# Strassen quarters for the i and z projections of heads 4 to 15, placed one product at a time among the t blocks

## The chip, the cores and the metric

One core of one Trainium2 chip runs the whole kernel in one launch. The metric is device time in microseconds (us). A core has a matrix engine (TensorE, PE in the profile; its weight loads are PEld), VectorE (DVE), ScalarE (ACT), GpSimd (POOL), the queue engine SyncE (SP), and 16 DMA engines that they share. Matmul results go to PSUM, which has eight banks of 128 x 512 floats here.

## The reference

A two-layer encoder on x of 512 tokens x 1024, in float32. Layer 0 is a gated MLP beside windowed attention. Layer 1, on which the change bears:

```
h = rms_norm(x, norm_g_odd);  proj = h @ w_in_odd              # 1024 -> 5 x 2048
q, f_f, f_b, i, z = split(proj)                                # 16 heads of 128 each
per head, both directions: f = lb + (1-lb)*sigmoid(f_logit), k = 1-f, in chunks of 64:
    S_t = diag(f_t) S_{t-1} + k_t outer i_t,   o_t = S_t^T silu(q_t)
o = rms_norm per head(o_fwd + o_bwd) * head_norm_g
x = x + (o * silu(z)) @ w_out_odd;   out = rms_norm(x, final_norm_g)
```

## The kernel before, in words

Every float32 product of a projection is made of three matmuls: each operand is split into a rounded high part and a low rest (hi, lo), and hi*hi, hi*lo and lo*hi are summed in PSUM (`mm3`, L212). One 128 x 128 by 128 x 512 step so costs three matmuls.

Weights come in pieces of 128 partitions x 1024 floats (512 KB) through `Weights` (L33). The list of pieces is written down once (L294 to L323) in the order of use. `take` hands out the next piece; `ahead` keeps up to 7 pieces requested and 3 split. A piece is loaded by SP into one of 4 `wraw` buffers (L55), ACT rounds it into `whi` (L66), and DVE subtracts to get `wlo` (L67); `whi` and `wlo` have 4 buffers each, so a split can wait for the matmuls that read an older piece.

Layer 1 goes in four groups J of four heads. For each group: `nat_blocks` computes i, then z, for the group's 512 columns (4 token tiles, 8 steps of three matmuls = 24 matmuls each; ACT copies i, L775; ACT sigmoid and DVE multiply make silu(z), L778 and L779); groups 1 and 2 then add the output projection of the group before (`out_blocks`, L260, added to x by DVE, L279); then each head computes q, f and b transposed (`t_block`, L220, 24 matmuls each, evacuated by ACT sigmoids, L790 and L794) and spawns `hgrn(h)` (L657). All these big blocks take their PSUM bank from the four-deep tag "mm" (L105); the heads' small matmuls use four "sm" banks.

`hgrn` is a generator. Its six pauses are counted in ticks: after every 8 matmuls of `mm3` one tick (L217) lets up to three such side jobs emit their next part. POOL has four steps in it: a memset (L663), the sum of two masked products (L708), the power -1/2 of the norm (L150), and the multiplication by silu(z) (L758). The written order is the priority; the framework's planner then puts each engine's instructions in the order in which its cost model finds them ready, and each engine runs its own list strictly in order.

After the last group come the output projections of heads 8 and 9, 10 to 13, and `last_blocks` (L799) with heads 14 and 15 and the final norm. The chip's first work is a chain on ACT: the first `hhi` (L348) and the first weight pieces.

Of the kernel before, what the change touches and what calls it, by code (L numbers as in the profile page):

```python
# [32 lines left out]
class Weights:  # L33
# [3 lines left out]
    def __init__(self, tc, pool, dma_ahead, split_ahead, raw_bufs, bufs):  # L37
        self.tc, self.nc, self.pool = tc, tc.nc, pool
        self.dma_ahead, self.split_ahead = dma_ahead, split_ahead
        self.raw_bufs, self.bufs = raw_bufs, bufs  # L40
        self.src, self.raw, self.ready = [], {}, {}
        self.n_dma = self.n_split = self.n_used = 0
        self.halved = 0

    def add(self, ap):
        self.src.append(ap)

    def _dma(self):
# [44 lines left out]
def tile_encoder(ctx, tc, x, xT, nge, wie, lng, lnb, ws, bs, sink, woe, ngo, wio, gaf, gab, hng, woo, fng, out):  # L93
# [17 lines left out]
    W = Weights(tc, wp, dma_ahead=7, split_ahead=3, raw_bufs=4, bufs=4)  # L111
# [171 lines left out]
    def act_pair():  # L283
        return [act.tile([P, S], F32R, tag=n, name=n, bufs=8) for n in ("ahi", "alo")]
# [38 lines left out]
    add_out(woo, 14, 2)  # L323

    with ExitStack() as c0:
# [95 lines left out]
        def layer_norm(t):  # L421
# [8 lines left out]
            nc.vector.tensor_tensor(out=va[t], in0=va[t], in1=lngb, op=ALU.mult)  # L430
            nc.gpsimd.tensor_tensor(out=va[t], in0=va[t], in1=lnbb, op=ALU.add)
# [338 lines left out]
    for J in range(4):  # L770
        iv = l1.tile([P, NT, 512], F32, tag="iv", name="iv", bufs=2)
        zv = l1.tile([P, NT, 512], F32, tag="zv", name="zv", bufs=2)
# [8 lines left out]
        nat_blocks(evac_i)  # L781
        nat_blocks(evac_z)
        if J in (1, 2):
            tick_until(lambda: 4 * J - 1 in acat1)
            out_blocks([acat1[4 * (J - 1) + k] for k in range(4)])
        for h in range(4 * J, 4 * J + 4):
            sq = l1.tile([P, 2, S], F32, tag="sq", name="sq", bufs=3)
            sg = l1.tile([P, 2, S], F32, tag="sg", name="sg", bufs=3)
# [106 lines left out]
```

## Time and profile before

| | |
|---|---|
| median of 3 runs | 1028.81 us (1028.78 to 1029.21) |
| the profiled execution's own time | 1028.67 us |
| its span, first to last instruction | 1027.0 us, so 1.67 us lie outside it |
| granted TensorE clock, mean | 0.998 |
| busy share PE, DVE, ACT, POOL | 98%, 59%, 51%, 13% |

Busy time of PE counts pipelined matmuls from their start to a modelled end, so matmuls overlap in it; the distance between two starts is what one costs. The other engines' busy time is occupancy. "DMA share" is the mean busy share of the core's 16 DMA engines.

### The profile page before, as it was taken

Reading aid. Unit: us, or ns where it says so; the run is one execution under the profiler, and the core shown is the slowest. Engines: PE = TensorE matmul, PEld = TensorE weight load, DVE = VectorE, ACT = ScalarE, POOL = GpSimd, SP = SyncE. Lnnn points to the kernel's source line nnn. Section 1 sums busy time; section 2 is a strip of 40 time slices with the busy share of each in tenths; the row PEclk is TensorE's granted clock in tenths of the full one; section 3 lists DMA queues with packets and bytes.
Section 4 is the critical chain, followed back from the end, with each engine's and each line's share of the span. In section 5 each row is a group of like instructions: output and inputs, shape, how many; then the busy total and the mean of one; then the engine's idle time right before and its main releaser. Section 6 shows DMA issues by size and latency. Waiting matters only on the chain.

```text
span 1027.0 us, 13567 instructions
## 1 busy us (share of the span) xinstructions
PE 1010.9 (98%) x5369; PEld 848.9 (83%) x5369; DVE 606.8 (59%) x976; ACT 521.4 (51%) x708; POOL 136.3 (13%) x155
## 2 busy tenths in 40 slices
PE   9999999999999999999999999999999999999996
PEld 6888888888888887888888888888888888888875
DVE  5575777575444464346754547754546764467775
ACT  6335666363222254368743258643358743587623
POOL 0320010022133300001220000120000121001112
PEclk9999999999999999999999999999999999999999
DMA  9443121322332313432202442202432213421102
GB/s 346 125 124 103 62 83 42 103 77 68 103 102 83 105 42 103 127 98 83 62 21 82 125 121 64 83 21 83 123 103 82 62 43 103 123 82 63 62 1 82
DMA packets 110527, 91.62 MB, mean 89 GB/s; under 512 B 3280, under 2 KB 88832, under 8 KB 110464
## 3 DMA queue, kind: packets, MB, share of 16 engines
q1 hardware_dynamic: 110224, 90.72, 28.6%
q8 instruction: 42, 0.69, 0.3%
q14 instruction: 21, 0.17, 0.1%
q0 software_dynamic: 96, 0.04, 0.0%
q10 hardware_dynamic: 144, 0.00, 0.0%
HBM read 88.65 MB, written 2.10 MB: 88 GB/s over the span
## 4 chain that ended last, share of the span: by engine, by line
PE 76%; ACT 10%; DVE 6%; issue 5%; POOL 1%; POOLq 0%; ACTq 0%; DVEq 0%
PE mm L215 64%; DVE c L671 2%; ACT L794 2%; ACT whi L66 2%; PE sm L500 1%; PE sm L727 1%; PE sm L539 1%; ACT L679 1%; ACT L665 1%; ACT c L665 1%; ACT en L679 1%; DVE wlo L67 1%; PE sm L742 1%; PE sm L699 1%; PE sm L746 1%
## 5 line engine op out<-in xcount | busy, mean ns | idle before, releaser
L66 ACT CAST whi<-wraw 128x1024 fp32r<-128x1024 f32 (+1 forms) x158 | 164.3, 1041 | 221.9 <-PE mm L215 188.8
L67 DVE TENSOR_TENSOR wlo<-wraw,whi 128x1024 fp32r<-128x1024 f32 (+1 forms) x158 | 200.4, 1272 | 109.8 <-ACT whi L66 107.8
L215 PE MATMUL mm<-hhi,wlo 128*128 128x512 f32 x656 | 257.7, 393 | 1.6 <-DVE wlo L67 1.6
L215 PE MATMUL mm<-hlo,whi 128*128 128x512 f32 x656 | 257.1, 392 | 0.0
L215 PE MATMUL mm<-hhi,whi 128*128 128x512 f32 x656 | 256.4, 391 | 0.0
L215 PEld LDWEIGHTS mm<-hhi,wlo 128*128 128x128 f32 x656 | 123.3, 188 | 26.1 <-DVE wlo L67 2.0
L215 PEld LDWEIGHTS mm<-hlo,whi 128*128 128x128 f32 x656 | 123.3, 188 | 24.5
L215 PEld LDWEIGHTS mm<-hhi,whi 128*128 128x128 f32 x656 | 123.3, 188 | 24.3
L215 PE MATMUL mm<-whi,hlo 128*128 128x512 f32 (+1 forms) x320 | 122.7, 383 | 0.0
L215 PE MATMUL mm<-wlo,hhi 128*128 128x512 f32 (+1 forms) x320 | 122.2, 382 | 0.3 <-DVE wlo L67 0.3
L215 PE MATMUL mm<-whi,hhi 128*128 128x512 f32 (+1 forms) x320 | 122.0, 382 | 0.0
L215 PE MATMUL mm<-whi,ahi 128*128 128x512 f32 (+1 forms) x258 | 100.7, 390 | 1.4 <-DVE x L279 1.4
L215 PE MATMUL mm<-whi,alo 128*128 128x512 f32 (+1 forms) x258 | 100.7, 390 | 0.0
L215 PE MATMUL mm<-wlo,ahi 128*128 128x512 f32 (+1 forms) x258 | 100.6, 390 | 0.0
L215 PEld LDWEIGHTS mm<-wlo,hhi 128*128 128x128 f32 x320 | 60.3, 188 | 12.1 <-DVE wlo L67 1.2
L215 PEld LDWEIGHTS mm<-whi,hhi 128*128 128x128 f32 x320 | 60.3, 188 | 10.6
L215 PEld LDWEIGHTS mm<-whi,hlo 128*128 128x128 f32 x320 | 60.3, 188 | 10.5
L279 DVE TENSOR_TENSOR x<-mm,x 128x512 f32<-128x512 f32 x64 | 43.8, 687 | 42.3 <-PE mm L215 42.2
L215 PEld LDWEIGHTS mm<-whi,ahi 128*128 128x128 f32 x258 | 48.5, 188 | 11.3 <-DVE x L279 1.8
L215 PEld LDWEIGHTS mm<-wlo,ahi 128*128 128x128 f32 x258 | 48.5, 188 | 9.5
L215 PEld LDWEIGHTS mm<-whi,alo 128*128 128x128 f32 x258 | 48.5, 188 | 9.5
L663 POOL MEMSET c<- 128x16 f32 x16 | 2.3, 152 | 341.0 <-DVE sq L689 341.0
(201 smaller groups left out, 1463.0 us busy)
## 6 DMA issues: line engine op xcount, KB each, us to landing
wraw<-in_w_in_odd_dram SPq DMA_DIRECT2D x80, 512.0 KB, 3.8
wraw<-in_w_in_even_dram SPq DMA_DIRECT2D x42, 512.0 KB, 3.8
wraw<-in_w_out_even_dram SPq DMA_DIRECT2D x16, 512.0 KB, 3.5
wraw<-in_w_out_odd_dram SPq DMA_DIRECT2D x16, 512.0 KB, 3.6
xk<-in_xT_dram SPq DMA_DIRECT2D x8, 256.0 KB, 5.5
x<-in_x_dram SPq DMA_DIRECT2D x4, 512.0 KB, 8.2
wraw<-in_w_in_even_dram SPq DMA_DIRECT2D x4, 256.0 KB, 4.7
out_dram<-x SPq DMA_DIRECT2D x4, 256.0 KB, 2.0
```

The source lines that it names most:

```text
L66: self.nc.scalar.copy(hi[:, j], raw[:, j])
L67: self.nc.vector.tensor_tensor(out=lo[:, j], in0=raw[:, j], in1=hi[:, j].bitcast(F32), op=ALU.subtract)
L215: nc.tensor.matmul(ps, lhsT=l, rhs=r, start=(i == 0), stop=(i == n - 1))
L279: nc.vector.tensor_tensor(out=xv, in0=ps, in1=xv, op=ALU.add)
L500: nc.tensor.matmul(pv, lhsT=a[:, ql], rhs=b[:, kv, kr], start=(i == 0), stop=(i == 2))
L539: nc.tensor.matmul(po[:, n0 * P:n1 * P], lhsT=a[:, j, ts(kv, P)], rhs=b[:, j, :w], start=(j == 0 and i == 0), stop=(j == NT - 1 and i == 2 ...
L665: nc.scalar.activation(c[:, d, :, 1:65], sg[:, d].rearrange("p (n t) -> p n t", t=64), AF.Ln, scale=oml[:, d, 0, h:h + 1], bias=lb[:, d, 0 ...
L671: nc.vector.tensor_tensor_scan(out=cf, data0=reset.rearrange("p n t -> p (n t)"), data1=cf, initial=0.0, op0=ALU.mult, op1=ALU.add)
L679: nc.scalar.activation(enf, cf, AF.Exp, scale=-1.0)
L699: nc.tensor.matmul(ps[:H, o:o + P], lhsT=kf[:, lo_:mid], rhs=qf[:, lo_:hi_], start=True, stop=True)
L727: nc.tensor.matmul(ps[:, ts(2 * j + d, P)], lhsT=kn[:, jj, d], rhs=iv[:, n, hs], start=True, stop=True)
L794: nc.scalar.activation(sg[:, d], ps, AF.Sigmoid)
```

## The change

The pairs of i and z of groups 1 to 3 (heads 4 to 15) are no longer two `nat_blocks`. The 1024 x 1024 weight of a group (i beside z) and h are cut in quarters, and seven products of quarters, in Winograd's form of Strassen's algorithm, replace eight. The sums of weight quarters (Z1, Y1, Y2, Y3) are formed by DMAs that POOL issues and that add to the raw piece already loaded (`accum_op`). The four sums of quarters of h are formed once by `make_forms`, stored to DRAM in split form, and loaded again for each product. `plan1` puts the products X1, X2, Z1, Z2, Y1, Y2, Y3 of the next group between the t blocks of the second and third pair of heads of the group before. The products sum in banks of the new tag "open": X2 goes on in the banks of X1, Z2 in those of Z1, Y2 and Y3 in those of Y1. t blocks of heads 0 to 11 have the other two banks.

Besides: five raw buffers and eight requests ahead; six buffers for the heads' outputs in place of eight; a small ACT copy at the very start; a pause ahead of POOL's add in layer 0's layer norm; three small loads from SP in place of POOL; one more tick in `hgrn`; the last output projections as heads 8 to 11, 12 and 13, 14 and 15.

```diff
-    def add(self, ap):
+    def add(self, ap, *more):
...
         n = len(self.src)
-        while self.n_dma < min(n, self.n_used + self.dma_ahead):
+        for entry in list(self.sums):
+            i, more = entry
+            if i < self.n_used + self.dma_ahead:
+                self.nc.gpsimd.dma_start(out=self.raw[i], in_=more.pop(0), accum_op=ALU.add)
+                if not more:
+                    self.sums.remove(entry)
+        while self.n_dma < min(n, self.n_used + self.dma_ahead + 1):
             self._dma()
...
-    pm = ctx.enter_context(tc.tile_pool(name="pm", bufs=4, space=bass.MemoryType.PSUM))
+    pm = ctx.enter_context(tc.tile_pool(name="pm", bufs=2, space=bass.MemoryType.PSUM))
+    turn = [0, True]
     def mm_bank():
-        return pm.tile([P, 512], F32, tag="mm", name="mm")
+        turn[0] += 1
+        return pm.tile([P, 512], F32, tag="mm" if turn[0] % 2 or not turn[1] else "open", name="mm")
+    def open_bank():
+        return pm.tile([P, 512], F32, tag="open", name="mm")
-    W = Weights(tc, wp, dma_ahead=7, split_ahead=3, raw_bufs=4, bufs=4)
+    W = Weights(tc, wp, dma_ahead=7, split_ahead=3, raw_bufs=5, bufs=4)
...
+        terms = {"X1": (b11,), "X2": (b21,), "Z1": (b11, b12), "Z2": (b22,), "Y1": (b11, b12, b22), "Y2": (b12, b22),
+                 "Y3": (b11, b12, b22, b21)}[name]
+        for p in range(2):
+            W.add(*[q[p] for q in terms])
...
+        u = [(n, J + 1) for n in ("X1", "X2", "Z1", "Z2", "Y1", "Y2", "Y3")]
+        plan1 += blocks[:6]
+        if J:
+            plan1 += [("out", h - 4)]
+        plan1 += u[:2] + blocks[6:7] + u[2:3] + blocks[7:8] + u[3:4] + blocks[8:9] + u[4:5] + blocks[9:10] + u[5:6] + blocks[10:] + u[6:]
...
+        early = small.tile([P, 1], F32, tag="early", name="early")
+        nc.gpsimd.memset(early, 0.0)
+        nc.scalar.activation(early, early, AF.Copy)
...
             nc.vector.tensor_tensor(out=va[t], in0=va[t], in1=lngb, op=ALU.mult)
+            yield 2
             nc.gpsimd.tensor_tensor(out=va[t], in0=va[t], in1=lnbb, op=ALU.add)
...
-        nc.gpsimd.dma_start(out=rows[32 * d:32 * d + 32], in_=gsrc.rearrange("l (h d) -> (l h) d", d=P))
+        nc.sync.dma_start(out=rows[32 * d:32 * d + 32], in_=gsrc.rearrange("l (h d) -> (l h) d", d=P))
...
-        pause = (7, 1, 1, 1, 1, 4) if h >= 14 else (8, 2, 2, 3, 2, 4)
+        pause = (7, 1, 1, 2, 1, 4) if h >= 14 else (8, 2, 2, 4, 2, 4)
...
+        def keep(i, s):
+            f = form_tile()
+            nc.scalar.copy(f[:, 0], s)
+            op(f[:, 1], s, f[:, 0].bitcast(F32), ALU.subtract)
+            nc.sync.dma_start(out=kept[i, p], in_=f.bitcast(F32))
...
+    def load_form(i, p):
+        f = form_tile()
+        nc.sync.dma_start(out=f.bitcast(F32), in_=kept[i, p])
+        return f
...
+    def silu(zv, t):
+        sig = l1.tile([P, 512], F32, tag="o2", name="sig", bufs=1)
+        nc.scalar.activation(sig, zv[:, t], AF.Sigmoid)
+        nc.gpsimd.tensor_tensor(out=zv[:, t], in0=zv[:, t], in1=sig, op=ALU.mult)
...
+        pieces = [W.take() for _ in range(2)]
+        first = name[1] == "1"
+        for p in range(2):
+            if first:
+                banks[name[0], p] = open_bank()
+            ps = banks[name[0], p]
...
+            for k in range(4):
+                (a, b), (whi, wlo) = a_of(k), pieces[k // 2]
+                ops += [(a, whi[:, k % 2]), (a, wlo[:, k % 2]), (b, whi[:, k % 2])]
+            mm3(ps, ops, first)
+            if name in NEXT:
+                loaded[NEXT[name], p] = load_form(FORM_OF[NEXT[name]], p)
+            if name == "X1":
+                nc.scalar.copy(iv[:, 2 + p], ps)
+            elif name == "X2":
+                nc.scalar.copy(iv[:, p], ps)
+            elif name == "Z1":
+                sub(zv[:, 2 + p], ps, iv[:, 2 + p])
+            elif name == "Z2":
+                sub(zv[:, p], ps, iv[:, 2 + p])
+            elif name == "Y1":
+                sub(zv[:, p], zv[:, p], ps)
+                silu(zv, p)
+            elif name == "Y2":
+                sub(zv[:, 2 + p], zv[:, 2 + p], ps)
+                silu(zv, 2 + p)
+            else:
+                nc.vector.tensor_tensor(out=iv[:, 2 + p], in0=ps, in1=iv[:, 2 + p], op=ALU.add)
...
+            if (kind, i) == ("X1", 1):
+                tick_until(lambda: len(formed) == 2)
+            product(i, kind)
...
-    tick_until(lambda: 9 in acat1)
-    out_blocks([acat1[8], acat1[9]])
+    tick_until(lambda: 11 in acat1)
+    out_blocks([acat1[k] for k in range(8, 12)])
     tick_until(lambda: 13 in acat1)
-    out_blocks([acat1[k] for k in range(10, 14)])
+    out_blocks([acat1[12], acat1[13]])
```

## Rows read from the trace of the kernel before

**Rows 1.** The page: span, busy time, PE and its clock by slice.
```profile
span 1027.0 us, 13567 instructions
PE 1010.9 (98%) x5369; PEld 848.9 (83%) x5369; DVE 606.8 (59%) x976; ACT 521.4 (51%) x708; POOL 136.3 (13%) x155
...
PE   9999999999999999999999999999999999999996
...
PEclk9999999999999999999999999999999999999999
```

**Rows 2.** The chain of waits around the start of group 2: start, us, what.
```profile
551.39 10.90 PE mm L215 x48
...
562.73 41.55 PE mm L215 x183
```

**Rows 3.** One group's period, the same four table loads apart: busy times, clock, DMA share, GB/s.
```profile
605.37:762.43 157.06, 156.59 (x874) 131.90 (x873) 90.09 (x140) 85.78 (x102) 15.68 (x20) 1.00 0.27 81
```

**Rows 4.** Start of the kernel, PE and ACT in time: start, us, engine, line, tiles [idle before].
```profile
1.53 4.45 PE L342 MATMUL sm<-warm 128*128 128x512 bf16 x10 [1.53 <-DVE warm L339]
...
3.58 1.28 ACT L348 ACT_TABLE_LOAD   x1 [3.58 <-DMA xk<-in_xT_dram]
...
6.16 0.57 PE L254 MATMUL mm<-whi,hhi 128*128 128x512 f32 x1 [0.18 <-ACT whi L66]
```

**Rows 5.** Layer norm of layer 0, POOL, DVE and PE in time.
```profile
48.44 2.40 POOL L431 TENSOR_TENSOR va<-va,lnbb 128x1024 f32<-128x1024 f32 x1 [2.25 <-DVE va L430]
50.79 0.56 POOL L150 TENSOR_TENSOR lnr<-lnv,mhalf 128x1 f32<-128x1 f32 x1
...
51.65 0.81 DVE L429 TENSOR_SCALAR va<-va,mv,lnr 128x1024 f32<-128x1024 f32 x1 [2.25 <-POOL lnr L427]
...
61.65 0.81 DVE L429 TENSOR_SCALAR va<-va,mv,lnr 128x1024 f32<-128x1024 f32 x1 [0.93 <-POOL lnr L427]
...
53.65 0.50 PE L215 MATMUL mm<-hhi,wlo 128*128 128x512 f32 x1 [1.58 <-DVE wlo L67]
```

**Rows 6.** Groups by line: busy us, mean ns | idle before, releaser.
```profile
L67 DVE TENSOR_TENSOR wlo<-wraw,whi 128x1024 fp32r<-128x1024 f32 x154 | 197.8, 1287 | 109.8 <-ACT whi L66 107.8
L66 ACT CAST whi<-wraw 128x1024 fp32r<-128x1024 f32 x154 | 161.9, 1052 | 221.8 <-PE mm L215 188.8 <-issue 30.4 <-DMA wraw<-in_w_in_even_dram 1.4
...
L779 DVE TENSOR_TENSOR zv<-mm,zv 128x512 f32<-128x512 f32 x16 | 11.0, 689 | 39.8 <-ACT zv L778 39.8
...
L775 ACT COPY iv<-mm 128x512 f32<-128x512 f32 x16 | 9.3, 582 | 26.6 <-PE mm L215 26.6
```

**Rows 7.** ACT beside head 1's start, in time.
```profile
475.51 1.28 ACT L679 ACT_TABLE_LOAD   x1 [1.84 <-DVE c L675]
476.81 1.07 ACT L679 ACTIVATE en<-c 128x1040 f32<-128x1040 f32 x1
...
479.01 1.28 ACT L790 ACT_TABLE_LOAD   x1
480.30 0.60 ACT L790 ACTIVATE sq<-mm 128x512 f32<-128x512 f32 x1
```

**Rows 8.** POOL in the same stretch, in time.
```profile
485.95 1.03 POOL L150 TENSOR_TENSOR hrr<-hrv,mhalf 128x4 f32<-128x4 f32 x1 [5.21 <-DVE hrv L145]
487.84 1.28 POOL L758 TENSOR_TENSOR o<-o,zv 128x512 f32<-128x512 f32 x1 [0.87 <-DVE o L757]
490.88 1.54 POOL L708 TENSOR_TENSOR asum<-asum,ax 64x256 f32<-64x256 f32 x2 [1.76 <-DVE asum L705]
```

**Rows 9.** The last two of POOL's three DMAs, of 32 and 16 rows, in time.
```profile
345.65 0.50 POOL L597 DMA_DIRECT2D rows<-in_hgrn_gamma_bwd_dram  x1
346.15 0.49 POOL L598 DMA_DIRECT2D rows<-in_hgrn_head_norm_g_dram  x1
```

**Rows 10.** DMA issues: KB each, median us from issue to landing.
```profile
wraw<-in_w_in_odd_dram SPq DMA_DIRECT2D x80, 512.0 KB, 3.8
```

More of the change, by code (lines that the diff above doesn't have):

```diff
@@ L56, in _dma @@
         self.raw[self.n_dma] = t
+        if more:
+            self.sums.append((self.n_dma, list(more)))
         self.n_dma += 1
@@ L210, in tick_until, with mm3 @@
             tick()
-    def mm3(ps, ops):
+    def mm3(ps, ops, first=True):
         n = len(ops)
         for i, (l, r) in enumerate(ops):
-            nc.tensor.matmul(ps, lhsT=l, rhs=r, start=(i == 0), stop=(i == n - 1))
+            nc.tensor.matmul(ps, lhsT=l, rhs=r, start=(first and i == 0), stop=(i == n - 1), skip_group_check=not first)
             count[0] += 1
@@ L283, in act_pair @@
     def act_pair():
-        return [act.tile([P, S], F32R, tag=n, name=n, bufs=8) for n in ("ahi", "alo")]
+        return [act.tile([P, S], F32R, tag=n, name=n, bufs=PAIRS) for n in ("ahi", "alo")]
     def split_act(src):
@@ L768, in hgrn, with quarter_of_h @@
         yield 1
[L770 to L772 removed]
+    spill = ctx.enter_context(tc.tile_pool(name="spill", bufs=1, space=bass.MemoryType.DRAM))
+    kept = {(i, p): spill.tile([P, 2, 4, P], F32, name=f"form{i}{p}", tag=f"form{i}{p}") for i in range(1, 5) for p in range(2)}
+    formed = set()
+    def quarter_of_h(a, th, kh, p):
+        return a[:, 4 * kh:4 * kh + 4, ts(2 * th + p, P)]
@@ new lines, in form_tile, with make_forms, op @@
+    def form_tile():
+        return l1.tile([P, 2, 4, P], F32R, tag="form", name="form", bufs=2)
+    def make_forms(p):
+        hi, lo = hhi.bitcast(F32), hlo.bitcast(F32)
+        q = lambda th, kh: (quarter_of_h(hi, th, kh, p), quarter_of_h(lo, th, kh, p))
+        a11, a12, a21, a22 = q(0, 0), q(0, 1), q(1, 0), q(1, 1)
+        s1, s2 = (l1.tile([P, 4, P], F32, tag=tag, name="s", bufs=1)[:] for tag in (("u", "kn1"), ("asum", "en"))[p])
+        def op(out, a, b, o):
+            nc.vector.tensor_tensor(out=out, in0=a, in1=b, op=o)
+        def keep(i, s):
[3 more added lines that the diff above has]
+            nc.sync.dma_start(out=kept[i, p], in_=f.bitcast(F32))
+        op(s1, a21[0], a22[0], ALU.subtract)
+        op(s2, a21[1], a22[1], ALU.subtract)
+        op(s1, s1, s2, ALU.add)
+        yield 1
+        keep(1, s1)
+        yield 1
+        op(s2, s1, a11[0], ALU.subtract)
+        op(s2, s2, a11[1], ALU.subtract)
+        yield 1
+        keep(2, s2)
+        yield 1
+        op(s2, s2, a12[0], ALU.add)
+        op(s2, s2, a12[1], ALU.add)
+        yield 1
+        keep(4, s2)
+        yield 1
+        op(s1, a11[0], a21[0], ALU.subtract)
+        op(s2, a11[1], a21[1], ALU.subtract)
+        op(s1, s1, s2, ALU.add)
+        yield 1
+        keep(3, s1)
+        formed.add(p)
+        yield 1
@@ L781, in tile_encoder @@
         nat_blocks(evac_i)
+        for p in range(2):
+            spawn(make_forms(p), 2)
         nat_blocks(evac_z)
[L783 to L788, printed above, removed]
+    cur = {}
+    for kind, i in plan1:
+        turn[1] = i >= 12
+        if kind == "nat":
+            turn[1] = True
+            first_group()
+        elif kind == "q":
+            cur["sq"] = l1.tile([P, 2, S], F32, tag="sq", name="sq", bufs=3)
+            cur["sg"] = l1.tile([P, 2, S], F32, tag="sg", name="sg", bufs=3)
+            sq = cur["sq"]
             ps = t_block()
```

79 lines of the change are left out of this document (61 added, 18 removed).

## The prediction

> **What bounds the kernel now.** Begin with the page's shares and slices: PE is busy 98% of the span and in tenths 9 in 39 of 40 slices, at a granted clock of full speed (2.4 GHz) throughout; DVE has 59%, ACT 51%, POOL 13% [rows 1]. Busy PE overcounts, so the chain of waits comes next. There PE runs 48 big matmuls in 10.90 us, 0.227 us each, start to start, and 183 in 41.55, again 0.227 [rows 2]. That is the price of a 128 x 512 matmul here, with its weight load beneath it. One whole group lasts 157.06 us [rows 3]: its 576 big matmuls (192 for i and z, 288 for twelve t blocks, 96 for the output) make 130.8 us, and the rest, 26.3 us, is the four heads' small matmuls. PE hardly waits inside it: the timeline shows waits for data of over 0.6 us only at the start, in the layer norm of layer 0 and at the end. So a big matmul removed is 0.227 us gained, as long as nothing that feeds PE becomes late.
>
> **The change part by part.**
>
> Matmuls. i and z of a group are 2 x 4 tiles x 24 = 192 matmuls; seven products are 7 x 2 token blocks x 12 = 168, of the same shape. Three groups save 72 x 0.227 = 16.3 us.
>
> The first ACT copy. ACT sits 3.58 us until the first x arrives and only then loads its table for 1.28 us [rows 4]; the copy puts the load into that wait. Of the 1.28 us PE can use less: its ten warm-up matmuls end at 5.98 and the first real one starts at 6.16 [rows 4]. Bounds 0.2 and 1.28; I take 0.3, nearest to the row.
>
> The pause in the layer norm. POOL's 2.40 us add stands ahead of the next token tile's power, DVE waits 2.25 us for that power, and PE then waits 1.58 us for a `wlo` queued behind on DVE [rows 5]. A tile without that add ahead of it cost DVE 0.93 [rows 5]. So 2.25 - 0.93 = 1.3 us come back, bounds 0 and 1.58. The late adds of POOL are needed only by the mixers much later.
>
> The three small loads on SP, 0.5 us each on POOL before [rows 9]: PE shows no wait there now; 0.
>
> Splits and evacuations. Fourteen pieces replace eight: 18 more splits, 18 x 1.05 = 18.9 us on ACT and 18 x 1.29 = 23.2 on DVE [rows 6]. z takes ten DVE subtractions and additions per group instead of four, 18 x 0.69 = 12.4 us [rows 6]. The sums of h are 28 DVE operations of that kind, 19 us, once, under 192 matmuls (44 us) of group 0. DVE comes to 607 + 55 = 662 us of some 1015, 65%; ACT with 19 of splits, some 12 of table loads (1.28 each, [rows 7]) and 8 copies to about 556, 55%. Both stay off the path as totals; I cost them at nothing, and what they cost locally is in the next two terms.
>
> X1 to X2. X2 sums on in X1's bank, so its first half needs ACT's 0.58 us copy [rows 6] within the 12 matmuls of X1's second half, 2.72 us. One split (1.05) ahead of it still fits; a table load and an exponential (1.28 + 1.07, [rows 7]) beside it do not, by up to 1.3 us. Six such places: 0 to 8 us, I take 1.8. What waits behind it on PE is X2 and then every head's small matmul.
>
> Two banks for t blocks in place of four. A t block's bank must be empty when the next but one starts, 5.45 us of matmuls later plus the small ones. ACT's order around a head's start, exponentials and table loads ahead of the sigmoid [rows 7], makes the evacuation late by about one block; the products between the later t blocks give slack, the first six of a group have none. 0 to 3 us a group, I take 0.5 each, 1.5.
>
> The outputs of groups 0 and 1. They now come 21 ticks after the last head was spawned, and its last part falls due in tick 23, so the pause is cut to two ticks, 16 matmuls, 3.6 us. The chain in it (square about 0.6, reduction 0.7, 0.2, power 1.03, product 0.7, product 1.28, [rows 6, 8]) takes 4.5. 0.8 us, twice: 1.6, unless the planner fills it. Bounds 0 and 9.
>
> The added-up weights. This is the open term. Each group has 14 adding DMAs of 512 KB issued by POOL, which no row shows. Issue: POOL's two later small DMAs took 0.50 us for 32 rows and 0.49 for 16 [rows 9], so rows hardly count: 42 x 0.5 = 21 us on an engine with 136 busy; by rows it would be 42 x 4 (256 rows) = 168. Landing: a plain piece takes 3.8 us [rows 10]. Engine time: 24 pieces in a group are 0.27 of 157.06 us [rows 3], 1.77 us of all 16 engines each. An adding DMA costs no less than that; its upper end is the point where it reads, adds and writes one after the other, three times, 5.3 us.
>
> Now the stage. A group has 552 big matmuls, 125.3 + 26.3 = 151.6 us, in 23 blocks of 24, 6.59 us a block with its small matmuls. From X1 to the start of Y3 there are twelve blocks, 79 us. In them the engines must carry 11 plain pieces, 8 stored forms of 512 KB (19 x 1.77 = 33.6 us) and 12 of the adding DMAs. 45.4 us are left, 3.8 for each, which is 2.1 plain ones. Below that the sums are in time on average. Y3 is the tightest: three sums in a row for each of two pieces after b8's raw buffer comes free; its second piece has Y1, b9, Y2, b10 and b11, 33 us, for a load (6.2 with its split ahead), three landings and the split (2.3). So a landing of up to 7.5 us with its issue is hidden. I take 1.5 plain ones (2.7 us of the engines, about 5 us to landing), nearer to the plain row than to its triple, and 1 us a group of lateness, 3.
>
> A rule that speaks against this is in the Trainium skill, "Collectives: The Full Stack", section "The bandwidth ceiling: the fold count and why AG ≠ RS ≠ AR": a DMA that adds reads two sources on one read ring and so runs at half the rate of a copy. By it the sum below would take the first rival's term (12 us) in place of my 3 us and come to 1028 us. No row here shows an adding DMA.
>
> Sum. 1028.67 (the profiled execution) - 16.3 - 0.3 - 1.3 = 1010.8 as the floor; + 1.8 + 1.5 + 1.6 + 3 = 1018.7. The 1.67 us outside the span are unchanged. The profiled execution lies 0.14 below the median of three, so I forecast 1018.5, rounded.
>
> **The rivals.**
>
> Twice a plain transfer. At 3.5 us each, 33.6 + 42.5 = 76 of 79 us still fit, but the last five blocks (33 us) hold 6 adding DMAs (21) and 9 plain ones (16): 4 us late a group, up to 12 in all in place of 3. 1018.7 + 9 = 1028, or less where plain ones wait instead: 1019 to 1031. For it: an add must read what it adds to. The Trainium skill's rule cited above gives this case. Against: at 0.27 the engines are mostly idle now [rows 3], and the plain pieces that compete are wanted only in the next group.
>
> The DMA engines become the bound (the other side). From 4.3 us per adding DMA on (33.6 + 12 x 4.3 = 85, 6 us over the 79, 18 in three groups), the gain is gone; at 5.3 it is 97 of 79, 54 us over: 1010.8 + 5 + 54 = 1070. The middle is 1050. For it: the triple bound. Against: a group as a whole would be busy 38 x 1.77 + 14 x 5.3 = 141 of 152, and nothing now comes near it.
>
> POOL stands in line. An adding DMA waits on POOL for the landing before it, and the heads' power and product [rows 8] wait behind. Their chain of 4.5 us has four ticks, 7.3 us, so a wait of 5 us makes PE 2.2 us late. At most eight heads have parts among the products: 18 us with the other terms, 1018.7 - 3 + 18 = 1034. For it: strict order. Against: POOL is 87% idle and the planner knows the loads' landings.
>
> The change does not save: only if products ran slower than 0.227 us a matmul; the operands have the same shapes, so I leave it at nothing.
>
> **How the numbers follow.** Forecast (1011 to 1022) 0.48; twice a plain transfer 0.24; DMA engines the bound 0.14; POOL in line 0.14. A measurement here tells 0.2%, 2 us, from no change. Faster: 0.48, two thirds of 0.24, a little of POOL's: 0.65. Within 2 us of 1028.8: 0.07. Slower: 0.28. The range 1010 to 1043 leaves out most of the DMA-bound case; the likeliest one's own is 1011 to 1022.
>
> **What would show it.** Right: 72 fewer big matmuls at 0.227 us; group periods near 152 to 155 us; no wait of 1.58 us in the layer norm; first real matmul just before 6 us; adding DMAs landing in 5 to 7 us. X1 to X2: PE idle released by ACT's copy. Two banks: PE idle released by sigmoids. DMA bound: `whi` released by DMAs and a DMA share near 0.9 beside the products. POOL in line: the power and product started long after DVE's release. I am wrong if one of the last two shows over 6 us a group, or if the three periods fall by less than 2 us each.

## The result: 7.7% slower, and the profile after

The changed kernel takes 1107.41 us in the median (1106.57 to 1111.67, four runs) beside 1028.85 for the kernel before: a ratio of 1.0771, 95% interval 1.0757 to 1.0785. The forecast was 1018.5 with a range of 1010 to 1043. The profiled execution has a span of 1105.0 us beside 1027.0 [rows 1]. Page of the changed kernel: span, busy time, slices, queues.

```profile
span 1105.0 us, 13794 instructions
PE 1017.0 (92%) x5297; PEld 848.7 (77%) x5297; DVE 660.2 (60%) x1040; ACT 549.6 (50%) x738; POOL 207.1 (19%) x207
...
PE   9999999999999999998769999759999965999997
...
PEclk9999999999999999999979999888999986999999
DMA  9352221323322256469932247992225996332102
...
q1 hardware_dynamic: 119856, 116.98, 33.1%
q0 software_dynamic: 11424, 22.02, 11.6%
```

PE has the 72 matmuls less (5369 in [rows 1]), and still 6 us more busy time, for the clock is no longer full. Its idle time, the span less the busy time, is 88.0 us, beside 16.1 before. The three dents of PE and of its clock stand where the DMA slices show 9 or just behind, in the second half of each group of products. POOL's queue q0 (the 42 adding DMAs) takes 11.6% of all 16 engines: 0.116 x 1105 / 42 = 3.05 us for each add. Where the time went, in windows of the changed kernel (stretch, length, busy time with instructions of PE, PEld, DVE, ACT, POOL, then granted clock, DMA share, GB/s):

```profile
0.00:480.00 480.00, 475.62 (x2321) 398.09 (x2322) 295.00 (x471) 226.40 (x350) 72.41 (x75) 1.00 0.38 119
480.00:562.00 82.00, 60.41 (x336) 49.53 (x335) 43.39 (x65) 36.39 (x45) 27.26 (x25) 0.89 0.88 216
562.00:950.00 388.00, 338.57 (x1785) 280.79 (x1785) 212.73 (x319) 197.74 (x228) 78.50 (x77) 0.93 0.56 143
```

Up to 480 us nothing is lost: the kernel before started 2322 matmuls in that stretch, this one 2321. From 480 to 562 us, in the first stage with products, the DMA engines are in use for 0.88 of the time, and PE for 60 of 82 us. (A group as a whole had 0.27 before, [rows 3].) The worst place in it, ACT in time (start, us, engine, line, tiles, [idle before <- releaser]):

```profile
537.83 1.04 ACT L70 CAST whi<-wraw 128x1024 fp32r<-128x1024 f32 x1
550.22 1.05 ACT L70 CAST whi<-wraw 128x1024 fp32r<-128x1024 f32 x1 [11.35 <-DMA wraw<-in_w_in_odd_dram]
556.78 0.63 ACT L889 ACTIVATE sig<-zv 128x512 f32<-128x512 f32 x1 [5.51 <-POOL zv L890]
559.98 1.05 ACT L70 CAST whi<-wraw 128x1024 fp32r<-128x1024 f32 x1 [2.56 <-DMA wraw<-in_w_in_odd_dram]
560.93 0.85 ACT L767 COPY kn<-sm 128x512 f32<-128x512 f32 x2
```

and POOL there:

```profile
524.26 1.24 POOL L89 DMA_DIRECT2D wraw<-in_w_in_odd_dram  x1 [3.20 <-DMA wraw<-in_w_in_odd_dram]
533.03 2.42 POOL L89 DMA_DIRECT2D wraw<-in_w_in_odd_dram  x2 [7.53 <-DMA wraw<-in_w_in_odd_dram]
...
540.97 1.22 POOL L89 DMA_DIRECT2D wraw<-in_w_in_odd_dram  x1 [4.19 <-DMA wraw<-in_w_in_odd_dram]
546.24 1.22 POOL L89 DMA_DIRECT2D wraw<-in_w_in_odd_dram  x1 [4.05 <-DMA wraw<-in_w_in_odd_dram]
554.25 1.20 POOL L89 DMA_DIRECT2D wraw<-in_w_in_odd_dram  x1 [6.80 <-DVE zv L883]
```

and PE's row at the end of it, with the same row of the other two groups:

```profile
561.56 1.22 PE L777 MATMUL sm<-iv,kn 128*128 128x128 f32 x4 [16.27 <-ACT kn L767]
...
746.54 0.80 PE L777 MATMUL sm<-iv,kn 128*128 128x128 f32 x2 [7.40 <-ACT kn L767]
...
930.72 0.58 PE L777 MATMUL sm<-iv,kn 128*128 128x128 f32 x1 [6.75 <-ACT kn L767]
```

Read from the bottom: PE stands 16.27 us for `kn`, which has nothing to do with the products. ACT copies `kn` at 560.93 because a split of weights stands ahead of it in ACT's fixed order, and that split waits for the group's last added-up piece. These are the last six adds of the group, Y3's two pieces with three each; POOL issues them over 30 us (524.26 to 554.25), each of the later ones behind the landing of one before it. The last wait of POOL names DVE: the add at 554.25 stands behind an operation that needs `zv`, DVE's `zv` stands behind a split that needs ACT's `whi`, and ACT waits for the DMA. So three fixed orders hold one another, but here this costs little: the add before it in the same piece had landed at 553.85, and DVE's `zv` was done at 554.18. The `kn` wait of the other two groups is shorter (7.40 and 6.75 us), with waits for a form (7.47, 7.57) and for `sq` (6.12, 6.70) beside it. From the end of one `kn` wait to the end of the next it is 185.0 and 184.2 us; a group's period was 157.06 [rows 3].

The DMA issues of the changed kernel (KB each, median us to landing) answer to [rows 10]:

```profile
wraw<-in_w_in_odd_dram SPq DMA_DIRECT2D x98, 512.0 KB, 4.4
...
wraw<-in_w_in_odd_dram POOLq DMA_DIRECT2D x42, 512.0 KB, 7.4
form<-form SPq DMA_DIRECT2D x32, 512.0 KB, 6.8
```

Plain pieces went from 3.8 to 4.4 us; an add lands in 7.4 (5.6 to 12.1), and each issue holds POOL for 1.2 us. The issues of the first group alone, from the first matmul of X1 (465.85 us) to the first of Y3 (572.58), and the window of that stage, show what the DMA engines had to carry there:

```profile
wraw<-in_w_in_odd_dram SPq DMA_DIRECT2D x18, 512.0 KB, 4.6
wraw<-in_w_in_odd_dram POOLq DMA_DIRECT2D x12, 512.0 KB, 8.0
form<-form SPq DMA_DIRECT2D x8, 512.0 KB, 7.1
...
465.85:572.58 106.73, 85.14 (x459) 70.82 (x458) 58.44 (x91) 52.08 (x64) 30.00 (x28) 0.90 0.78 195
```

The 12 adds and 8 forms are those of the prediction, but the plain pieces are 18, not its 11: pieces requested ahead for what follows Y3 are loaded here too. 0.78 of 106.73 us is 83 us of all 16 engines, in a stage that the prediction gave 79.

### The profile page after: what moved, and what is told of

It is laid out like the page before. It is cut to its first block, busy times and chain, and to the rows that moved or that the text cites. A ratio compares the mean times of both kernels' runs of the same rounds, so it can differ in the third digit from the quotient of the medians.

```text
span 1105.0 us, 13794 instructions
## 1 busy us (share of the span) xinstructions
PE 1017.0 (92%) x5297; PEld 848.7 (77%) x5297; DVE 660.2 (60%) x1040; ACT 549.6 (50%) x738; POOL 207.1 (19%) x207
## 3 DMA queue, kind: packets, MB, share of 16 engines
q0 software_dynamic: 11424, 22.02, 11.6%
## 4 chain that ended last, share of the span: by engine, by line
PE 61%; issue 12%; DMA 9%; DVE 8%; ACT 6%; POOL 4%; POOLq 0%; ACTq 0%; DVEq 0%
PE mm L233 50%; DMA wraw<-in_w_in_odd_dram 9%; PE sm L777 2%; DVE wlo L71 2%; PE sm L550 1%; PE sm L589 1%; ACT whi L70 1%; DVE c L721 1%; PE sm L792 1%; POOL wraw L89 1%; ACT L729 1%; PE sm L578 1%; ACT en L729 1%; PE sm L749 1%; ACT L968 1%
## 5 line engine op out<-in xcount | busy, mean ns | idle before, releaser
L70 ACT CAST whi<-wraw 128x1024 fp32r<-128x1024 f32 (+1 forms) x176 | 183.0, 1042 | 300.9 <-PE mm L233 206.1
L71 DVE TENSOR_TENSOR wlo<-wraw,whi 128x1024 fp32r<-128x1024 f32 (+1 forms) x176 | 217.8, 1242 | 135.7 <-ACT whi L70 134.6
L233 PE MATMUL mm<-hlo,whi 128*128 128x512 f32 x656 | 260.9, 398 | 0.0
L89 POOL DMA_DIRECT2D wraw<-in_w_in_odd_dram x42 | 51.2, 1255 | 216.4 <-DMA wraw<-in_w_in_odd_dram 164.9
L233 PE MATMUL mm<-whi,form 128*128 128x512 f32 x192 | 66.1, 416 | 15.0 <-DMA form<-form 15.0
L233 PE MATMUL mm<-wlo,hhi 128*128 128x512 f32 (+1 forms) x200 | 75.0, 376 | 0.3 <-DVE wlo L71 0.3
L233 PE MATMUL mm<-whi,hhi 128*128 128x512 f32 (+1 forms) x200 | 75.2, 376 | 0.0
L233 PE MATMUL mm<-whi,hlo 128*128 128x512 f32 (+1 forms) x200 | 74.6, 374 | 0.0
L233 PEld LDWEIGHTS mm<-whi,form 128*128 128x128 f32 x192 | 38.3, 199 | 25.8 <-ACT c L715 15.8
L233 PEld LDWEIGHTS mm<-whi,alo 128*128 128x128 f32 x258 | 48.5, 188 | 11.5 <-DVE alo L815 2.0
L777 PE MATMUL sm<-iv,kn 128*128 128x128 f32 x192 | 28.5, 306 | 30.4 <-ACT kn L767 30.4
```

Of the source, the lines that this page charges most:

```text
L70: self.nc.scalar.copy(hi[:, j], raw[:, j])
L71: self.nc.vector.tensor_tensor(out=lo[:, j], in0=raw[:, j], in1=hi[:, j].bitcast(F32), op=ALU.subtract)
L89: self.nc.gpsimd.dma_start(out=self.raw[i], in_=more.pop(0), accum_op=ALU.add)
L233: nc.tensor.matmul(ps, lhsT=l, rhs=r, start=(first and i == 0), stop=(i == n - 1), skip_group_check=not first)
L777: nc.tensor.matmul(ps[:, ts(2 * j + d, P)], lhsT=kn[:, jj, d], rhs=iv[:, n, hs], start=True, stop=True)
```

## The experiments

The theory tested: the adding DMAs make the whole loss, by landing late and by standing in POOL's order. Rivals: the traffic of the stored forms, the side edits, or the new order of stages itself.

**Without the adds (e1).** The products use one quarter in place of the sum.

```
-            W.add(*[q[p] for q in terms])
+            W.add(terms[0][p])
```

> Leaves out the 42 adding DMAs, so Z1, Y1, Y2 and Y3 use one quarter of the weights instead of a sum; all else as in the changed kernel. Theory A (the adding DMAs carry the loss: they fill the DMA engines and land too late): 1010 to 1022 us, no wait of ACT's whi for a DMA. Theory B (the loss is in the rest of the new order: two banks for t blocks, stored forms, evacuations): above 1080 us, with PE still stopped some 16 us in the first product stage.

1028.8 us (1025.29 to 1030.42), ratio 0.9993 (0.9982 to 1.0004). The adds cost 78.6 us; the rest of the change gains nothing although 16.3 us of matmuls are gone, so the time lies above the 1010 to 1022 of theory A. No ACT wait for a DMA is left in the product stages. What is left shows in PE's, POOL's and DVE's rows of this run:

```profile
568.72 0.55 PE L812 MATMUL sm<-ident,o 128*128 128x128 f32 x3 [2.69 <-POOL o L808]
...
562.13 1.01 POOL L168 TENSOR_TENSOR hrr<-hrv,mhalf 128x4 f32<-128x4 f32 x1 [19.22 <-DVE hrv L163]
...
565.12 0.69 DVE L739 TENSOR_TENSOR sq<-sq,c 128x512 f32<-128x512 f32 x1
565.73 0.68 DVE L807 TENSOR_TENSOR o<-sm,hrr 128x512 f32<-128x512 f32 x1
```

and in its windows:

```profile
565.00:575.00 10.00, 7.31 (x56) 5.72 (x55) 5.32 (x9) 6.20 (x8) 2.24 (x2) 0.83 0.15 55
```

The wait of 2.69 us for the output's product returns in each group, and the granted clock of the 10 us around it is 0.83. DVE does the next head's four products first and the output's own at 565.73, though the power that this needs was done at 563.14.

**Small adds (e2).** Each add covers 64 of 512 columns, so the sums are incomplete in the others.

```
-                self.nc.gpsimd.dma_start(out=self.raw[i], in_=more.pop(0), accum_op=ALU.add)
+                self.nc.gpsimd.dma_start(out=self.raw[i][:, :, :64], in_=more.pop(0)[:, :, :64], accum_op=ALU.add)
```

> Keeps all 42 adding DMAs, with their waits and their places on POOL, but each adds 64 of 512 columns (64 KB in place of 512 KB), so the sums are incomplete. Theory A1 (bytes: the engines' time per adding DMA, 3.05 us of all 16 in the changed kernel, fills the stage): 1012 to 1030 us. Theory A2 (strict order and the chain of up to three landings, each about 2 us even when small, with POOL's 1.2 us per issue): above 1060 us.

1054.1 us, 1.0242 (1.0219 to 1.0265), between the two theories: an eighth of the bytes keeps 25 of the 79 us. The adds use 3.0% of the DMA engines, but still land only after 4.5 us. POOL of this run:

```profile
489.87 1.20 POOL L89 DMA_DIRECT2D wraw<-in_w_in_odd_dram  x1 [5.95 <-DMA wraw<-in_w_in_odd_dram]
492.74 1.22 POOL L89 DMA_DIRECT2D wraw<-in_w_in_odd_dram  x1 [1.67 <-DMA wraw<-in_w_in_odd_dram]
494.03 1.04 POOL L168 TENSOR_TENSOR hrr<-hrv,mhalf 128x4 f32<-128x4 f32 x1
```

and DVE:

```profile
488.16 0.17 DVE L163 TENSOR_SCALAR hrv<-hss 128x4 f32<-128x4 f32 x1
495.10 0.69 DVE L807 TENSOR_TENSOR o<-sm,hrr 128x512 f32<-128x512 f32 x1 [6.77 <-POOL hrr L168]
```

The power's input is there at 488.33; the power starts at 494.03, behind two adds that wait for landings. PE loses 5.24 us there, for DVE's `o`. This is the rival "POOL in line" at work. It is not all of e2's loss: ahead of the `kn` wait of the same group, 3.11 us, a split still waits 1.65 us for a DMA.

**Plain copies in place of adds (e3).** Same bytes to the same buffers, without adding, so each piece holds its last quarter alone.

```
-                self.nc.gpsimd.dma_start(out=self.raw[i], in_=more.pop(0), accum_op=ALU.add)
+                self.nc.gpsimd.dma_start(out=self.raw[i], in_=more.pop(0))
```

> The same 42 DMAs of 512 KB from POOL, but as plain copies over the raw piece (the sums are not formed): same bytes from HBM, same chain, no second read. If the second read of an add is what fills the engines: engine time near 1.7 us each and 1015 to 1045 us. If landing chain and order on POOL decide, whatever an add costs: above 1075 us.

1069.53 us, 1.0392 (1.0376 to 1.0407), again between the two. The queue line of this run is

```profile
q0 software_dynamic: 6048, 22.02, 6.2%
```

0.062 x 1067 / 42 = 1.58 us of the engines each, 5.8 us to landing. An add at 3.05 us costs 1.93 times that. The Trainium skill, "Collectives: The Full Stack", section "The bandwidth ceiling: the fold count and why AG ≠ RS ≠ AR", says of the transfers that add in a ReduceScatter that they read two sources and so run at half the rate of the copies of an AllGather; the ratio of this pair of runs agrees. The two queue lines show it as packets: 11424 for the adds and 6048 for the copies of the same 22.02 MB, at about the same engine time each. That a second reading makes the difference, no row shows. From e2 to e3 it is 15 us, from e3 to the changed kernel another 38. These 38 us are the price of adding in place of copying, not of the engine time alone, for the issue of a plain copy also holds POOL for only 0.72 us.

**The forms loaded once (e4).** 22 of 24 loads of stored forms of h are left out, and the two that stay serve all products.

```
-        f = form_tile()
-        nc.sync.dma_start(out=f.bitcast(F32), in_=kept[i, p])
-        return f
+        if p not in once:
+            once[p] = form_tile()
+            nc.sync.dma_start(out=once[p].bitcast(F32), in_=kept[i, p])
+        return once[p]
```

> Loads two stored forms once and uses them for every product (wrong forms), so 22 of 24 loads of 512 KB go, some 1.64 us of all 16 engines each, 36 us in all; the adding DMAs stay. If the fullness of the DMA engines in the product stages is the cause, the adds land earlier and the time falls by 25 to 70 us, to 1040 to 1080. If the chain of adds alone decides, only PE's own waits for forms go, about 15 us: 1088 to 1097 us.

1088.61 us, 1.0569 (1.0533 to 1.0605): 11.5 MB less beside the adds give back 19 us. PE's waits for a form and for `sq` are gone, and the `kn` waits stay or grow (13.62, 17.00, 14.92 us). The forms add to the crowd and do not make it.

**POOL freed of arithmetic (e9, e10).** The product of silu, the sum into `asum` and o times z go to DVE; e9 with small adds (incomplete as in e2), e10 with the full ones.

```
-        eng = nc.vector if h >= 14 else nc.gpsimd
+        eng = nc.vector
...
-            nc.gpsimd.tensor_tensor(out=av, in0=av, in1=ax[lo_:lo_ + H], op=ALU.add)
+            nc.vector.tensor_tensor(out=av, in0=av, in1=ax[lo_:lo_ + H], op=ALU.add)
...
-        nc.gpsimd.tensor_tensor(out=zv[:, t], in0=zv[:, t], in1=sig, op=ALU.mult)
+        nc.vector.tensor_tensor(out=zv[:, t], in0=zv[:, t], in1=sig, op=ALU.mult)
```

> The kernel of e2 (adding DMAs of 64 of 512 columns, so the sums are left incomplete in 448 columns) with POOL's arithmetic, the product of silu, the sum into asum and o times z, moved to DVE; on POOL only the power of hrr and the transfers remain. Theory (POOL in line: work that others wait for stands behind an adding DMA that waits for the transfer before it): the waits of TensorE of 3 to 5 us at kn, sq and o go, and the time falls from 1054 to 1029 to 1038 us, with DVE busier by some 60 us. Rival (the landing itself is late, whoever computes): it stays at 1050 to 1058. Second rival (DVE is now the strict line): slower than 1058.

> The changed kernel whole (full adding DMAs) with the same operations of POOL moved to DVE. If POOL's order alone made the loss, the time falls from 1107 to 1030 to 1045 us. If the landing of the sums at 7.4 us and the DMA engines at one full use behind it make it, ACT's whi split still waits for DMA about 10 us before kn and the time stays above 1075 us. Between them: both, in the share that the time shows.

e9: 1045.06 us, 1.0154 (1.013 to 1.0177), 9 us less than e2 and 7 above the upper end of what was expected; PE's wait of 4.65 us from 488 on stays, since the power still stands behind an add. e10: 1101.66, 1.0709 (1.0694 to 1.0724), only 6 us less than the changed kernel. ACT of e10:

```profile
548.68 1.04 ACT L70 CAST whi<-wraw 128x1024 fp32r<-128x1024 f32 x1 [13.89 <-DMA wraw<-in_w_in_odd_dram]
...
559.11 1.04 ACT L70 CAST whi<-wraw 128x1024 fp32r<-128x1024 f32 x1 [8.86 <-DMA wraw<-in_w_in_odd_dram]
560.06 0.85 ACT L767 COPY kn<-sm 128x512 f32<-128x512 f32 x2
```

In this stretch (522 to 563 us) no wait of POOL names DVE any more, only DMAs, and ACT waits longer, 13.89 and 8.86 us. The late landing, with the chain of adds still issued one behind the other by POOL, is enough for nearly all of the loss; POOL's arithmetic was the smaller part.

**An earlier start of the chain (e13, e14).** One raw buffer more and one piece more of lead; e13 in the changed kernel, e14 in e10.

```
-    W = Weights(tc, wp, dma_ahead=7, split_ahead=3, raw_bufs=5, bufs=4)
+    W = Weights(tc, wp, dma_ahead=8, split_ahead=3, raw_bufs=6, bufs=4)
```

> The changed kernel with six raw buffers in place of five and transfers eight pieces ahead in place of seven, so every plain transfer and every add may start one piece (24 matmuls, 5.45 us) earlier. Theory (the chain starts too late): ACT's wait for the sums of Y3, 9 to 14 us per group, falls by about 5.5 us, with the waits behind it and the clock some 8 to 10 us for each of three groups: 1107 to 1078 to 1090 us. Rival (the pace of the adds in POOL's one line, at DMA engines in full use, is the limit): the same time within 5 us, 1102 to 1110. A third way: the adds come earlier into POOL's order, and o times z and the power stand behind them: slower, 1112 to 1125.

> e10 (POOL free of the silu product, asum and o times z) with the same buffer and lead as e13. Theory: from 1102 to 1070 to 1082 us, and further down than e13, since nothing but the power of hrr stands in POOL's line. Rival (pace): 1097 to 1103 us.

e13: 1097.93 us, 1.065 (1.0623 to 1.0678), 9.5 less than the changed kernel; e14: 1089.98, 1.0588 (1.0572 to 1.0603), 11.7 less than e10. Both lie between theory and rival. ACT's two waits in e14 are 12.47 and 2.01 us where e10 had 13.89 and 8.86: the lead is used. But the adds now take 8.4 us (e13) and 8.8 us (e14) to land. And a new wait stands among the first products, 6.66 us in e13 and this one in e14, where a head's power stands behind the earlier adds on POOL:

```profile
495.26 0.45 PE L765 MATMUL sm<-ident,sg 128*128 128x128 f32 x1 [6.33 <-DVE o L807]
```

That is the third way of the expectation, in one place. Windows of e14, and behind them one of the changed kernel:

```profile
500.00:520.00 20.00, 20.00 (x106) 16.89 (x105) 11.81 (x20) 9.02 (x10) 5.01 (x4) 0.99 0.87 220
520.00:540.00 20.00, 20.00 (x90) 16.33 (x89) 15.37 (x21) 14.89 (x17) 4.86 (x5) 1.00 0.93 260
540.00:550.00 10.00, 7.33 (x60) 5.72 (x59) 2.44 (x3) 1.31 (x2) 1.87 (x2) 1.00 1.10 275
...
540.00:550.00 10.00, 5.30 (x44) 4.25 (x40) 1.48 (x2) 0.00 (x0) 2.43 (x2) 0.87 1.10 276
```

(A packet is counted whole in the window in which it starts, so a share can exceed 1.) In e14 the engines are nearly full from 500 us on, while PE runs without a stop until 547. So the pace of the transfers in this stretch limits as well as the late start, and more lead is partly eaten by longer landings.

**The sums formed in layer 0 (e6).** 24 copies and 24 adds between DRAM tensors, issued by POOL during layer 0; the pieces of the products are then plain loads. Y1 is formed from Z1 and Y3 from Y1, so fewer adds are needed than the 42.

```
+            s = sp0.tile([P, 2, 512], F32, name=f"sum{name}{j}{p}", tag=f"sum{name}{j}{p}")
...
+            W.add(s[:])
...
+                if acc:
+                    nc.gpsimd.dma_start(out=dst[:], in_=src_ap, accum_op=ALU.add)
+                else:
+                    nc.gpsimd.dma_start(out=dst[:], in_=src_ap)
...
+            ins = nc.gpsimd.tensor_tensor(out=z, in0=zt, in1=z, op=ALU.mult)
+            issue_sums(ins.ins, 5 if tag == "zb" else 1)
```

> The changed kernel, but the sums of weight quarters are formed during layer 0 between DRAM tensors, by 24 copies and 24 adding DMAs that POOL issues one to five at a time behind its own work; the pieces are then loaded as plain ones. If only the time and place of the adds cost (they fill the DMA engines and stop ACT in the product stages), this comes to the time without sums, 1028.8 us, plus what layer 0 loses, 0 to 6 us. If adding DMAs cost whatever stands beside them: above 1060 us.

1028.76 us (1025.64 to 1030.59), 0.9990 (0.9982 to 0.9999). The windows of layer 0 in the kernel before and in this run:

```profile
0.00:480.00 480.00, 476.18 (x2322) 398.21 (x2323) 278.24 (x445) 220.59 (x339) 69.84 (x75) 1.00 0.34 104
...
0.00:480.00 480.00, 475.79 (x2313) 398.31 (x2314) 294.05 (x469) 224.13 (x348) 108.33 (x121) 1.00 0.60 168
```

The DMA share rises from 0.34 to 0.60 there and PE loses nothing by it (e1, without any add, starts 2311 matmuls in this stretch). The adds take 6.5 to 12.4 us to land and nobody waits for them: the same sums, formed elsewhere, cost nothing against e1 instead of 78.6 us. So forming the sums isn't what costs; forming them in the raw buffers among the products is. The run moves the adds, makes fewer of them and takes the chains out of the raw buffers, all at once; it doesn't tell these three apart. The same 2.7 us waits as in e1 remain.

**Its pauses tuned (e7).** e6 without the pause in the layer norm, and with the last pause of a head's output 6 in place of 4 ticks.

```
-            yield 2
-        pause = (7, 1, 1, 2, 1, 4) if h >= 14 else (8, 2, 2, 4, 2, 4)
+        pause = (7, 1, 1, 2, 1, 4) if h >= 14 else (8, 2, 2, 4, 2, 6)
```

> The same with two local edits: no pause in the layer norm, and the last pause of hgrn for heads 0 to 13 six ticks instead of four, so that the transposes that PE waits 2.7 us for, once a group (POOL's product is late because DVE runs Y3's work and the next head's start first), stand 16 matmuls later. If these waits and the lower clock behind them are what is left over the saved matmuls: 9 to 14 us below the run without them, 1016 to 1022 us. If the rest is spread over many small delays: less than 4 us.

1018.64 us (1018.49 to 1019.15), 0.9897 (0.9883 to 0.9911), 10.1 us less than e6. The three waits of 2.7 us for o times z are gone, with the lower clock around the first two (565 to 575 us: 0.83 in e6, 1.00 in e7). In exchange there are four new waits of 0.87 to 0.90 us, for `alo` and `u`, and the last output's wait is 0.5 us shorter. The other edit is no part of it: PE's wait in the layer norm is 2.0 us in both runs, and the pause alone changes nothing (e8).

**The side edits (e5, e8).** On the kernel before: e5 has the early copy, the pause and the small loads on SP; e8 the pause alone.

```
+        early = small.tile([P, 1], F32, tag="early", name="early")
+        nc.gpsimd.memset(early, 0.0)
+        nc.scalar.activation(early, early, AF.Copy)
...
+            yield 2
...
-    nc.gpsimd.dma_start(out=rows[64:80], in_=hng[0].rearrange("(h d) -> h d", d=P))
+    nc.sync.dma_start(out=rows[64:80], in_=hng[0].rearrange("(h d) -> h d", d=P))
```

> The kernel before with the side edits alone: the first ACT copy, the pause in the layer norm, the three small loads from SP. The prediction's terms would make it 1.6 us faster, 1027.2 us. The trace of the changed kernel speaks against: the order on POOL is the same there, and PE waits 2.04 us at that place, after which the clock is at 0.69 for 5 us; by that it is 0.5 to 2 us slower than before.

> The kernel before with the pause in the layer norm alone. If the planner puts POOL's instructions in the same order either way: no change, within 0.3 us of 1028.9. If the pause works as written: 1.3 us faster.

e5: 1030.55 us in the median, 1.0008 (1.0000 to 1.0017). e8: 1028.86, 0.9999 (0.9990 to 1.0008). Neither gains. e5's eleven runs fall in two: five at 1028.85 to 1029.38 with a mean granted clock of 0.998, six at 1030.55 to 1031.47 with 0.996 or 0.997. (The clock of 0.69 that its expectation ascribes to the changed kernel stands in e1's trace, 55 to 60 us; the changed kernel's own trace has 1.00 there, behind a wait of 2.04 us.) POOL's order in the layer norm is unchanged by the pause, as the changed kernel's own rows show beside [rows 5]:

```profile
48.15 2.41 POOL L481 TENSOR_TENSOR va<-va,lnbb 128x1024 f32<-128x1024 f32 x1 [2.25 <-DVE va L479]
50.52 0.55 POOL L168 TENSOR_TENSOR lnr<-lnv,mhalf 128x1 f32<-128x1 f32 x1
```

**Without the early copy (e11), and the add really put later (e12),** both on e7.

```
-        early = small.tile([P, 1], F32, tag="early", name="early")
-        nc.gpsimd.memset(early, 0.0)
-        nc.scalar.activation(early, early, AF.Copy)
```

```
-            nc.gpsimd.tensor_tensor(out=r, in0=r, in1=rq[:, t:t + 1], op=ALU.mult)
+            ins = nc.gpsimd.tensor_tensor(out=r, in0=r, in1=rq[:, t:t + 1], op=ALU.mult)
+            if t:
+                with tc.issue_after(ins.ins):
+                    nc.gpsimd.tensor_tensor(out=va[t - 1], in0=va[t - 1], in1=lnbb, op=ALU.add)
...
-            yield 2
-            nc.gpsimd.tensor_tensor(out=va[t], in0=va[t], in1=lnbb, op=ALU.add)
+            if t == NT - 1:
+                nc.gpsimd.tensor_tensor(out=va[t], in0=va[t], in1=lnbb, op=ALU.add)
```

> e7 without the early copy on ACT at the start. The prediction gave that copy a gain of 0.3 us. Theory: TensorE starts earlier but then waits longer in the layer norm, at a lower granted clock in 50 to 60 us, so without the copy the time is the same or up to 1 us shorter than e7: 1017.5 to 1018.8 us. Rival: the copy is worth its 0.3 us, 1018.9 to 1019.3.

> e7 with POOL's layer-norm add of one tile put behind the power of the next tile in POOL's order, which is what the pause was meant to do. Theory: TensorE's wait of 2.0 us at 51 us goes and the clock stays at full in 50 to 60 us, 1.5 to 3 us less than e7: 1015.5 to 1017.2. Rival: the wait moves to DVE's next operation or to the out projection's tiles and the time stays at 1018 to 1019.

e11: 1015.82 us (1015.73 to 1016.17), 0.9873 (0.9860 to 0.9887), the fastest of all, 2.8 us below e7 where at most 1 was expected. PE's wait in the layer norm and window 50 to 60 us of e7:

```profile
53.53 0.80 PE L234 MATMUL mm<-hhi,wlo 128*128 128x512 f32 x1 [2.01 <-DVE wlo L71]
...
50.00:60.00 10.00, 7.99 (x28) 6.21 (x27) 8.47 (x7) 2.32 (x3) 4.65 (x4) 0.83 0.50 142
```

of e11:

```profile
53.85 0.50 PE L234 MATMUL mm<-hhi,wlo 128*128 128x512 f32 x1 [1.57 <-DVE wlo L71]
...
50.00:60.00 10.00, 8.43 (x38) 6.66 (x37) 8.15 (x7) 3.84 (x5) 5.00 (x4) 1.00 0.44 127
```

and the window of the changed kernel, whose wait is 2.04 us:

```profile
50.00:60.00 10.00, 7.96 (x35) 6.25 (x35) 8.62 (x8) 3.22 (x4) 4.51 (x4) 1.00 0.51 144
```

With the copy PE starts at 5.40 us in place of 6.36, then waits 2.01 us in the layer norm, and the granted clock of the window is 0.83; without it the wait is 1.57 us, the clock stays full, and ten more matmuls are started in the window, 2.3 us. The lower clock doesn't follow from the wait alone. Of the twelve traces with the copy and a wait of 2.0 us, six have 0.83 in this window (e1, e2, e5, e6, e7, e10) and six have 1.00 (the changed kernel, e3, e4, e9, e13, e14); the three with a wait of about 1.58 us (the kernel before, e8, e11) all have 1.00. Matmul by matmul, e7 is 0.8 us ahead of e11 before this wait and 1.3 behind at 62 us. The further 1.5 us up to the end come in small steps over the whole rest of the kernel, and nothing here ties them to the copy.

e12: 1020.95 us, 0.992 (0.9906 to 0.9933), 2.3 us slower than e7 where a gain was expected. The order is as meant, but DVE now does its scaling beside POOL's add. DVE of e12:

```profile
51.47 2.82 DVE L509 TENSOR_SCALAR va<-va,mv,lnr 128x1024 f32<-128x1024 f32 x1 [0.93 <-POOL lnr L504]
```

POOL of e12:

```profile
51.38 2.35 POOL L507 TENSOR_TENSOR va<-va,lnbb 128x1024 f32<-128x1024 f32 x1
```

DVE's wait for the power fell from 2.25 to 0.93, just as the prediction had it, and the operation behind it takes 2.82 us in place of 0.81 [rows 5], ending 0.56 after POOL's. PE's wait grew from 2.01 to 3.44. The Trainium skill, "SBUF — State Buffer", section "SBUF: two separate sides", says that DVE in some modes and POOL take a shared pair of ports for a whole instruction while the other stands; these rows agree, but for the 0.25 us by which DVE ends sooner than 0.81 us after POOL.

## Why the prediction was wrong

**The step that failed is the term of the added-up weights: 3 us forecast, 78.6 measured (e1, e6).** Its parts:

- Engine time: taken 2.7 us an add, limits 1.77 to 5.3; measured 3.05. This was in the range, and by the prediction's own balance (33.6 + 12 x 3.05 = 70 of 79 us) nothing would be late on average.
- The balance itself: it counted 11 plain pieces from X1 to Y3 where the trace has 18, so the measured transfers fill 83 us, more than the 79 of the stage. That sum alone is 4 us a group. And it was an average over twelve blocks, when 12 of a group's 14 adds belong to Y1, Y2 and Y3 at its end: the share was 0.88 in 480 to 562 us and 1.10 in 540 to 550.
- Landing: taken 5 us, with 7.5 as the limit of what is hidden for Y3; the median is 7.4 and the longest 12.1. A chain of three was costed as three landings, with 24.5 us for them (33 less 6.2 and 2.3). In the trace one POOL issues two such chains in turn, each add behind a wait, the last three starts are 5.3 and 8.0 us apart, and from the first start to the split that takes the last sum (524.26 to 559.98) it is 35.7 us.
- Issue: taken 0.5 us by rows of small DMAs [rows 9]; measured 1.2. 42 x 0.7 = 29 us more of POOL, whose own weight no run shows apart.
- What a late sum stops: the prediction made only the product late. In fact the split that waits for it stands in ACT's order ahead of the head's `kn`, so PE stops for both.
- The clock: in PE's stop of 16.27 us the window 550 to 562 was granted 0.50, the lower level (1.2 GHz), and 562 to 600 still had 0.92. The prediction had no term for it. PE's busy time shows it: 1017.0 us against 999.7 in e7 with the same number of matmuls.

So the loss of 78.6 us against e1, some 26 a group, is 4 by the bare sum of the transfers; the rest goes with their crowding at the end of the stage, the late chain, what stands behind it and the clock. Of the rivals none was right by itself. "DMA engines the bound" had the right signs (`whi` released by DMAs, a DMA share near 0.9) at 3.05 us an add, well below its threshold of 4.3, and its upper price of 1070 was too low. "POOL in line" is what e2 shows. "Twice a plain transfer" had the right engine time (1.93, e3) and the wrong price, 1028. They were priced as alternatives; they came together, and each wait was lengthened by the others.

**The other terms.** Matmuls: right. With the sums out of the way the group period is 154.2 us in e11 (158.0 in e1), within the 152 to 155 that were forecast for it. e11 has 1015.82, and its floor, 1010.8 plus the two gains that did not come (0.3 and 1.3), is 1012.4. Of the remaining 3.4 us, 2.7 are of the size of PE's waits of over 0.6 us that are new in it: 0.84 and 0.90 twice, for `alo` and `u`, and 1.31 for the last output, 4.8 in all, less the 0.78 and 1.35 that the kernel before has near its end. X1 to X2 and the two banks: forecast 3.3, and no PE wait of either kind is seen in e11; 0. Outputs' pause: forecast 1.6 within 0 to 9; e7 shows some 10, since the planner put the next head's products ahead on DVE, in three places rather than two, with the clock on top of it. Layer-norm pause: forecast −1.3, measured 0 (e8): it did not move the add, and where the add was moved (e12) DVE lost the time beside POOL. Early copy: forecast −0.3; e7 loses 1.3 us by it up to 62 us, of its 2.8 against e11, and by its ratio e5 loses 0.8 with it and the two other edits. Chance of slower: 0.28, with prices up to 1070; the time itself lay beyond every case.

What stays open: how the 79 us divide between late start and the engines' pace. Lead was tried by one piece only; fewer adds in the same place (24 for 42, as in e6), and an order of products with the sums spread more evenly, weren't tried.

## What to carry to other kernels

Balance transfers over the stretch in which they are wanted, not over a group, with those requested ahead for later work counted in, and follow a chain of dependent DMAs through the queue that issues it, link by link. Before a load with a wait is put into an engine's fixed order, look at what stands behind it there: the price of a late load is the first unrelated thing that the order holds up, plus the clock that PE loses while it stands. The remedy was not a faster sum but another place: the same sums, formed where nobody waits for them and the DMA engines have room (a share of 0.34), cost nothing. Of the 16 us of matmuls 10 then showed in e7 and 13 in e11.

## What the runs showed of the hardware

- An adding DMA of 512 KB took 3.05 us of all 16 DMA engines, a plain one from the same queue 1.58 (the changed kernel and e3), in 11424 and 6048 packets for 42 of them; an adding one of 64 KB still took 4.5 us to land (e2).
- The issue of an adding DMA holds POOL 1.21 us, at 512 KB and at 64 KB alike; the issue of a plain one of 512 KB holds it 0.72 us (e3).
- Short waits of PE can cost more than their length: without three of 2.7 us, and with four new ones of 0.9, e7 is 10.1 us below e6, and the clock of 565 to 575 us went from 0.83 to 1.00.
- The same short wait lowered the granted clock in some executions and not in others: of twelve traces with a wait of 2.0 us in the layer norm, six had 0.83 in 50 to 60 us and six 1.00. The runs of e5 fall in two groups some 2 us apart, with mean clocks of 0.998 and 0.996 to 0.997.
- A DVE scaling of 128x1024 that took 0.81 us alone took 2.82 and 2.87 beside a POOL add of 2.35 and 2.40 (e12).
